# Starting the tiles that TensorE reads at multiples of 256 bytes in SBUF

## The chip, the cores and the metric

The kernel runs on one core of a Trainium2 chip. The metric is device time in microseconds (us): the median of the runs of one program. Beside it stands one profiled execution, with its own time and its span (first to last instruction).

## The reference

One layer of a streaming encoder, for 256 prompt frames and 32 frames of a running stream, so 288 token columns in all, with `D_MODEL` = 2048 and everything in float32:

```python
h = rms_norm(x, g_pre) * (1.0 + scale[:, None]) + shift[:, None]
proj = h @ w_in                      # (2048) x (2048 * 9)
gb, gc, gu, zc, q, k, v, zr, ma, mb = jnp.split(proj, SPLIT_POINTS, axis=-1)
y_conv = gb * causal_conv3(gc * gu) * silu(zc)
y_ret = headRMS(retention(rope(q), rope(k), v)) * silu(zr)
merged = sigmoid(ma) * (y_conv @ w_branch[0]) + sigmoid(mb) * (y_ret @ w_branch[1])
x = x + gate[:, None] * rms_norm(merged @ w_out, g_post)
```

`scale`, `shift` and `gate` come from `silu(c) @ ada_w + ada_b`; new convolution and retention states are also returned.

## The kernel before

**Split products.** The products run in float32r. To keep float32 accuracy each operand is split in a high part (ScalarE copy, L116) and a low part (VectorE subtract, L117). A weight block of 1 MB is loaded into `raw` (L131), split in pieces of 1,024 columns into `whi` and `wlo`, and used by `accumulate` (L151, L152, L154): for each of the k-tiles of a piece, `whi` against the activation's high part, `whi` against its low part, and later `wlo` against the high part. The weights are the stationary operand (128 columns); the activations `hh`/`hl` (later `yh`/`yl`, `ch`/`cl`, `mh`/`ml`) are the moving one (288 columns). There are 9,216 such matmuls of 288 columns, three for each of 3,072 pairs of k-tile and output tile.

**Stages.** (1) `x` is loaded, normalised and transposed (L264); `modulation` (L280) multiplies `ada_w` as a moving operand of 512 columns by a small `cs`; `first_products` computes the first q, k and v columns group by group. (2) The retention loop: `product` for the rest of q, k, v and z, with the steps of `attend` (L397 to L399: `vh`, `vl`, `stateh`, `statel` moving, 256 columns) pushed between them by `step`. (3) The m_b product and the branch of the retention. (4) The convolution branch. (5) m_a, the other branch, and (6) `w_out` with the final norm. TensorE's order is that of the program; weight loads go out on SP's queue, whatever is small on ACT's.

**Where tiles begin.** Pools take SBUF one after the other, each tile from where the last ended, rounded up to 32 bytes. The first tile of the kernel begins at byte 16,512 of each partition. A tile of 288 float32 columns per k-tile, as `hh`, has slices of 1,152 bytes, that is 4.5 x 256, so that its slices begin in turn at two places modulo 256. Starts modulo 256, of the tiles in the argument:

| tile (read by TensorE as) | before | after |
|---|---|---|
| `raw`, `whi`, `wlo` in pool `wp` (weights) | 32 | 0 |
| the extra `raw`, `whi`, `wlo` of pool `start` (buffers 5 and 6 of 6, first stage only) | 0 | 0 |
| `hh`, `hl`, `mh`, `ml`, slices of k even / odd (moving) | 32 / 160 | 0 / 128 |
| `yh`, `yl`, `ch`, `cl`, slices of k even / odd (moving) | 160 / 32 | 0 / 128 |
| `vh`, `vl` (moving, 256 columns) | 128 | 0 |
| `ident`, `gh`, `gl`, `ones` | 128, 160, 160, 160 | 0 |

In the first stage a split piece takes the buffers of `wp` four times and those of `start` twice, in turn (`buffer`, L121 to L125).

Of the kernel before, what the change touches and what calls it, by code (L numbers as in the profile page):

```python
# [10 lines left out]
F32 = mybir.dt.float32  # L11
# [5 lines left out]
P = 128  # L17
D = 2048
NK = D // P
# [5 lines left out]
NH = 8  # L25
# [17 lines left out]
NR = 8  # L43
# [10 lines left out]
PB = dict(v=2, kd=1, pr=1, state=1, qs=1)  # L54
FV = 2 * (len(FIRST) - 2)

DC = TP + P + TS


def tables():  # L60
# [10 lines left out]
    def dec(n):  # L71
        return np.exp((lg.reshape((NH,) + (1,) * np.ndim(n)) * np.asarray(n, f)[None]).astype(np.float64))
# [3 lines left out]
    full = dec(np.abs(j - i)) * (j // CHUNK <= i // CHUNK)  # L76
    d = np.zeros((P, NH, DC), f)
    d[:, :, :TP] = full[:, :P, :].transpose(1, 0, 2)
# [15 lines left out]
def hybrid_step(ctx: ExitStack, tc, x_prompt, x_sample, c_prompt, c_sample, state_conv, state_ret,  # L94
# [4 lines left out]
    V, A, G = nc.vector, nc.scalar, nc.gpsimd  # L99

    const = ctx.enter_context(tc.tile_pool(name="const", bufs=1))
    wp = ctx.enter_context(tc.tile_pool(name="wp", bufs=2))
    big = ctx.enter_context(tc.tile_pool(name="big", bufs=1))
    tmp = ctx.enter_context(tc.tile_pool(name="tmp", bufs=2))
    acc = ctx.enter_context(tc.tile_pool(name="acc", bufs=4, space=PSUM))
    aux = ctx.enter_context(tc.tile_pool(name="aux", bufs=4, space=PSUM))

# [6 lines left out]
    def split(src, hi, lo):  # L114

        A.copy(out=hi, in_=src)  # L116
        V.tensor_tensor(out=lo, in0=src, in1=hi.bitcast(F32), op=ALU.subtract)  # L117
# [48 lines left out]
    def product(w, col, xh, xl):  # L166
# [10 lines left out]
                next(later, None)  # L177
        return [o[:, :T] for o in out]

    ident = const.tile([P, P], F32, name="ident")  # L180
    make_identity(nc, ident)
    neghalf = const.tile([P, 3], F32, name="neghalf")
    V.memset(neghalf, -0.5)
    ones32 = const.tile([P, P], F32, name="ones32")
    V.memset(ones32, 1.0)
    ones = const.tile([P, P], F32R, name="ones")
    V.tensor_copy(ones, ones32)

    def rstd_of(ss, n, width):

        m = tmp.tile([P, 3], F32, name="ms", tag="ms")
        V.tensor_scalar(out=m[:, :width], in0=ss, scalar1=1.0 / n, scalar2=EPS, op0=ALU.mult, op1=ALU.add)
        r = tmp.tile([P, 3], F32, name="rstd", tag="rstd")
        G.tensor_tensor(out=r[:, :width], in0=m[:, :width], in1=neghalf[:, :width], op=ALU.pow)
        return r


    vecs = const.tile([P, NR, NK], F32, name="vecs")
    hh = big.tile([P, NK, T], F32R, name="hh", tag="hh")
    hl = big.tile([P, NK, T], F32R, name="hl", tag="hl")  # L200
    cs = const.tile([P, NK, 12], F32R, name="cs")
    sc = const.tile([P, NK, 2], F32, name="sc")

    early = ExitStack()
    fpool = early.enter_context(tc.tile_pool(name="firsts", bufs=1, side="right", reuse_waits="tile"))
    firsts = fpool.tile([P, 4 * len(FIRST), T], F32, name="firsts")

    rows_of = (P, P, TS)
    with tc.tile_pool(name="start", bufs=1, reuse_waits="tile") as st:
# [25 lines left out]
        V.tensor_tensor(out=sc, in0=cv, in1=sg, op=ALU.mult)  # L235
        V.memset(cs.bitcast(F32), 0.0)
        split(sc, cs[:, :, 4:6], cs[:, :, 6:8])
        ab1 = st.tile([P, NK], F32, name="ab1")
        V.tensor_scalar(out=ab1, in0=vp[:, 2 * NK:3 * NK], scalar1=1.0, scalar2=None, op0=ALU.add)
        xT = st.tile([P, NK, T], F32, name="xT")  # L240

# [4 lines left out]

        def norm_x():

            ss = st.tile([P, 3], F32, name="ss")
            V.memset(ss, 1.0)  # L250
            for g in range(3):
                n = rows_of[g]
                junk = xT.rearrange("p k t -> p (k t)")[:, g * T:g * T + D]
                A.activation(junk[:n], x[:n, g, :], AF.Square, accum_out=ss[:n, g:g + 1])  # L254
            rx = rstd_of(ss, D, 3)
            for g in range(3):
                n = rows_of[g]
                V.tensor_scalar(out=x[:n, g, :], in0=x[:n, g, :], scalar1=rx[:n, g:g + 1], scalar2=None, op0=ALU.mult)
# [81 lines left out]
        h0 = make_h(*GROUPS[0])  # L340
        load_x()
        norm_x()
        for k in range(2):
            turn_x(k)
# [24 lines left out]
    with tc.tile_pool(name="ret", bufs=2, reuse_waits="tile") as rp:  # L369
        rope = rp.tile([P, 2, T], F32, name="rope", bufs=1)  # L370
        A.dma_start(out=rope, in_=rope_t)
        kdec = rp.tile([P, NH, 3], F32, name="kdec", bufs=1)
        A.dma_start(out=kdec, in_=kdec_t)
        qdec = rp.tile([P, NH, TS], F32, name="qdec", bufs=1)
        A.dma_start(out=qdec, in_=qdec_t)
# [16 lines left out]
        def parts(shape, name):  # L392
            return [rp.tile(shape, F32R, name=name + p, bufs=PB[name]) for p in ("h", "l")]

        def add_product(ps, a, b, ai, bi, first, last):

            nc.tensor.matmul(ps, a[0][ai], b[0][bi], start=first, stop=False)  # L397
            nc.tensor.matmul(ps, a[0][ai], b[1][bi], start=False, stop=False)  # L398
            nc.tensor.matmul(ps, a[1][ai], b[0][bi], start=False, stop=last)  # L399
# [18 lines left out]
        def attend(h, q, k, vt, zs):  # L418
# [2 lines left out]
            A.dma_start(out=state, in_=state_ret[0, 0, h])  # L421
            state2 = parts([P, DV], "state")
            split(state, *state2)
            dec = rp.tile([P, DC], F32, name="dec", bufs=1)
            A.dma_start(out=dec, in_=dec_t[:, h, :])

            pk = aux_tile()
# [23 lines left out]
            nc.tensor.matmul(psc[:, 0:TP], k[:, 0:P], q[:, 0:TP], start=True, stop=True)  # L451
            nc.tensor.matmul(psc[:, TP:TP + P], k[:, P:TP], q[:, P:TP], start=True, stop=True)
            nc.tensor.matmul(psc[:TS, TP + P:DC], k[:, TP:T], q[:, TP:T], start=True, stop=True)
            pr = rp.tile([P, DC], F32, name="pr", bufs=1)
            V.tensor_tensor(out=pr[:, :TP + P], in0=psc[:, :TP + P], in1=dec[:, :TP + P], op=ALU.mult)
            V.tensor_tensor(out=pr[:TS, TP + P:], in0=psc[:TS, TP + P:DC], in1=dec[:TS, TP + P:], op=ALU.mult)
            pr2 = parts([P, DC], "pr")
            split(pr[:, :TP + P], pr2[0][:, :TP + P], pr2[1][:, :TP + P])
# [23 lines left out]
            add_product(po[:, DV:2 * DV], pr2, v, (every, slice(TP, TP + P)), (every, 1), False, True)  # L482
            add_product(ps[:TS, 0:DV], qs2, state2, (every,), (every,), True, False)
            add_product(ps[:TS, 0:DV], pr2, v, (few, slice(TP + P, DC)), (few, 2), False, True)
            so = rp.tile([P, 3], F32, name="so")
            V.memset(so, 1.0)
            on = rp.tile([P, 3, DV], F32, name="on", bufs=1)
            src = (po[:, 0:DV], po[:, DV:2 * DV], ps[:TS, 0:DV])
            for g in range(3):
                n = rows_of[g]  # L490
                A.activation(on[:n, g, :], src[g], AF.Square, accum_out=so[:n, g:g + 1])
            ro = rstd_of(so, DV, 3)
            for g in range(3):
                n = rows_of[g]
# [12 lines left out]
        for hp in range(NH // 2):  # L507
            qr = turned(O_Q, 0, "q", hp)
            kr = turned(O_K, 1, "k", hp)
            for f in range(2):  # L510
                h = 2 * hp + f
                v = values(h)
                zs = gates(h)
                while len(side) > 1:
                    step()
                side.append(attend(h, qr[f], kr[f], v, zs))
# [68 lines left out]
    with tc.tile_pool(name="cnv", bufs=2, reuse_waits="tile") as cp:  # L585
        last = cp.tile([P, NK, 4], F32, name="last", bufs=1)
        for q in range(NQ):
# [8 lines left out]
            for f in range(2):  # L596
                kt = 2 * q + f
                g = cp.tile([P, GW], F32, name="g")
# [57 lines left out]
    with tc.tile_pool(name="fin", bufs=2, reuse_waits="tile") as fp:  # L656
        so = fp.tile([P, 3, NQ], F32, name="so", bufs=1)
# [70 lines left out]
```

## Time and profile before

| | us |
|---|---|
| median of 3 runs | 1391.85 (1390.7 to 1396.4) |
| profiled execution, its time | 1392.17 |
| its span | 1390.4 |
| TensorE busy with matmuls, in the span | 1358.9 |
| VectorE, ScalarE busy | 872.3, 611.6 |

A matmul's row gives its start, and a length of some 0.29 us that overlaps with the next; so the cost of one matmul in a stream is read from the distance between two starts. The busy time of TensorE tells only that it hardly ever stood still.

### The profile page before, as it was taken

To read this page: it belongs to the slowest core of one execution; us is meant where nothing else is said; L and a number is where in the kernel's file an instruction comes from. 1 tells how busy PE (TensorE), PEld (TensorE's weight loads), DVE (VectorE), ACT (ScalarE), POOL (GpSimd) and SP (SyncE) were. 2 spreads that over 40 slices of the span, in tenths; PEclk is the share of its full clock that TensorE was granted. 3 is DMA by queue.
4 is the path that set the end of the run, shared out by engine and by line. 5 is a ranking of instruction groups with operands and counts; after the bars stand their busy time and mean duration, and the time that the engine had idled before them with its cause. 6 is when DMAs were issued, how large, how long until landed. Compare 5 with 4: busy or idle time off the path is not lost.

```text
span 1390.4 us, 23832 instructions
## 1 busy us (share of the span) xinstructions
PE 1358.9 (98%) x9978; PEld 1300.1 (94%) x9978; DVE 872.3 (63%) x1426; ACT 611.6 (44%) x885; POOL 9.2 (1%) x16
## 2 busy tenths in 40 slices
PE   4999999999999999999999999999999999999996
PEld 1677899999999999999999999999999999999996
DVE  5888976655545757566767767776555334555443
ACT  6876645544444333333333333333333333334442
POOL 0000000000000000000000000000000000000000
PEclk9999999999999999999999999999999999999998
DMA  9988854344445566575656666566545455557431
GB/s 334 334 302 310 303 175 156 121 158 156 149 159 165 169 196 207 191 241 181 220 185 214 194 202 199 183 201 211 172 155 171 161 171 163 167 168 232 156 105 69
DMA packets 234068, 267.79 MB, mean 193 GB/s; under 512 B 5076, under 2 KB 208132, under 8 KB 233348
## 3 DMA queue, kind: packets, MB, share of 16 engines
q1 hardware_dynamic: 227968, 256.22, 55.8%
q10 hardware_dynamic: 5992, 10.04, 2.7%
q8 instruction: 78, 1.28, 0.4%
q14 instruction: 30, 0.25, 0.0%
HBM read 261.75 MB, written 4.49 MB: 191 GB/s over the span
## 4 chain that ended last, share of the span: by engine, by line
issue 66%; PE 31%; DVE 1%; DMA 0%; ACT 0%; SPq 0%; POOL 0%; DVEq 0%; POOLq 0%; ACTq 0%
PE acc L151 8%; PE acc L154 8%; PE acc L152 8%; PE aux L280 4%; PE aux L397 1%; PE aux L264 1%; PE aux L398 1%; PE aux L399 1%; PE aux L502 0%; DMA x<-in_x_prompt_dram 0%; DVE wlo L117 0%; DVE x L697 0%; PE aux L443 0%; PE aux L451 0%; ACT xT L254 0%
## 5 line engine op out<-in xcount | busy, mean ns | idle before, releaser
L117 DVE TENSOR_TENSOR wlo<-raw,whi 128x1024 fp32r<-128x1024 f32 x448 | 542.1, 1221 | 384.4 <-ACT whi L116 383.8
L116 ACT CAST whi<-raw 128x1024 fp32r<-128x1024 f32 x448 | 464.3, 1050 | 562.8 <-PE acc L152 530.1
L151 PE MATMUL acc<-hh,whi 128*128 128x288 f32 x2304 | 632.1, 296 | 0.0
L152 PE MATMUL acc<-hl,whi 128*128 128x288 f32 x2304 | 631.2, 295 | 0.0
L151 PEld LDWEIGHTS acc<-hh,whi 128*128 128x128 f32 x2304 | 432.5, 188 | 5.0 <-issue 1.7
L152 PEld LDWEIGHTS acc<-hl,whi 128*128 128x128 f32 x2304 | 433.2, 188 | 0.9 <-DVE hl L117 0.3
L154 PE MATMUL acc<-hh,wlo 128*128 128x288 f32 x2304 | 405.4, 293 | 0.0
L154 PEld LDWEIGHTS acc<-hh,wlo 128*128 128x128 f32 x2304 | 340.9, 188 | 0.0
L542 DVE SCALAR_TENSOR_TENSOR gbc<-raw,sc,gbc 128x256 f32<-128x256 f32 x240 | 100.3, 476 | 13.5 <-DMA raw<-in_ada_w_dram 13.5
L152 PE MATMUL acc<-ml,whi 128*128 128x288 f32 x256 | 71.1, 298 | 0.0
L151 PE MATMUL acc<-mh,whi 128*128 128x288 f32 x256 | 70.9, 300 | 0.0
L151 PE MATMUL acc<-yh,whi 128*128 128x288 f32 x256 | 70.0, 296 | 0.0
L152 PE MATMUL acc<-yl,whi 128*128 128x288 f32 x256 | 70.0, 295 | 0.0
L151 PE MATMUL acc<-ch,whi 128*128 128x288 f32 x256 | 70.0, 296 | 0.0
L152 PE MATMUL acc<-cl,whi 128*128 128x288 f32 x256 | 69.5, 294 | 0.0
L280 PE MATMUL aux<-wlo,cs 128*8 128x512 f32 x128 | 51.3, 401 | 0.3
L280 PE MATMUL aux<-whi,cs 128*8 128x512 f32 x128 | 51.6, 403 | 0.0
L151 PEld LDWEIGHTS acc<-mh,whi 128*128 128x128 f32 x256 | 48.3, 189 | 0.1
L152 PEld LDWEIGHTS acc<-cl,whi 128*128 128x128 f32 x256 | 48.3, 189 | 0.0
L152 PEld LDWEIGHTS acc<-ml,whi 128*128 128x128 f32 x256 | 48.1, 188 | 0.1
L152 PEld LDWEIGHTS acc<-yl,whi 128*128 128x128 f32 x256 | 48.2, 188 | 0.0
L151 PEld LDWEIGHTS acc<-yh,whi 128*128 128x128 f32 x256 | 48.1, 188 | 0.1
(188 smaller groups left out, 963.8 us busy)
## 6 DMA issues: line engine op xcount, KB each, us to landing
raw<-in_w_in_dram SPq DMA_DIRECT2D x144, 1024.0 KB, 5.1
raw<-in_ada_w_dram SPq DMA_DIRECT2D x48, 1024.0 KB, 6.5
raw<-in_w_branch_dram SPq DMA_DIRECT2D x32, 1024.0 KB, 5.6
raw<-in_w_out_dram SPq DMA_DIRECT2D x16, 1024.0 KB, 5.6
x<-in_x_prompt_dram SPq DMA_DIRECT2D x2, 1024.0 KB, 5.9
out_dram<-ns SPq DMA_DIRECT2D x16, 128.0 KB, 5.7
x<-in_x_prompt_dram ACTq DMA_DIRECT2D x1, 2048.0 KB, 8.0
out_dram<-x ACTq DMA_DIRECT2D x4, 512.0 KB, 2.8
```

The costliest lines, as they stand in the source:

```text
L116: A.copy(out=hi, in_=src)
L117: V.tensor_tensor(out=lo, in0=src, in1=hi.bitcast(F32), op=ALU.subtract)
L151: nc.tensor.matmul(ps, hi[:, k, fs], xh[:, k0 + k, :], start=first and k == 0, stop=False)
L152: nc.tensor.matmul(ps, hi[:, k, fs], xl[:, k0 + k, :], start=False, stop=False)
L154: nc.tensor.matmul(ps, lo[:, k, fs], xh[:, k0 + k, :], start=False, stop=last and k == n - 1)
L264: nc.tensor.transpose(out=px[:, g * P:g * P + n], in_=x[:n, g, k * P:(k + 1) * P], identity=ident[:n, :n])
L280: nc.tensor.matmul(pm[:8, :width], cs[:, kt, rows_at], w[:, k, :], start=(part == 0 and kt == 0 and w is hi), stop=(part == 1 and kt == NK ...
L397: nc.tensor.matmul(ps, a[0][ai], b[0][bi], start=first, stop=False)
L398: nc.tensor.matmul(ps, a[0][ai], b[1][bi], start=False, stop=False)
L399: nc.tensor.matmul(ps, a[1][ai], b[0][bi], start=False, stop=last)
L542: V.scalar_tensor_tensor(out=ga[:, b], in0=raw[:, k], scalar=sc[:, kt, b:b + 1], in1=ga[:, b], op0=ALU.mult, op1=ALU.add)
```

## The change

Fillers and wider small tiles move the starts; no instruction is added or taken away but in the sizes of tiles. `LINE` is 64 floats (256 bytes), `OFFSET` 32 floats (128 bytes, which takes the first tile from 16,512 to 16,640 = 65 x 256).

```diff
+LINE, OFFSET = 64, 32
...
     const = ctx.enter_context(tc.tile_pool(name="const", bufs=1))
+    tmp = ctx.enter_context(tc.tile_pool(name="tmp", bufs=2))
     wp = ctx.enter_context(tc.tile_pool(name="wp", bufs=2))
     big = ctx.enter_context(tc.tile_pool(name="big", bufs=1))
-    tmp = ctx.enter_context(tc.tile_pool(name="tmp", bufs=2))
...
+    const.tile([P, OFFSET], F32, name="offset")
     ident = const.tile([P, P], F32, name="ident")
-    neghalf = const.tile([P, 3], F32, name="neghalf")
+    neghalf = const.tile([P, LINE], F32, name="neghalf")[:, :3]
-    ones32 = const.tile([P, P], F32, name="ones32")
+    vecs = const.tile([P, NR, NK], F32, name="vecs")
+    ones32 = vecs.rearrange("p r k -> p (r k)")
...
-        m = tmp.tile([P, 3], F32, name="ms", tag="ms")
+        m = tmp.tile([P, LINE], F32, name="ms", tag="ms")
-        r = tmp.tile([P, 3], F32, name="rstd", tag="rstd")
+        r = tmp.tile([P, LINE], F32, name="rstd", tag="rstd")
...
-    sc = const.tile([P, NK, 2], F32, name="sc")
+    sc = const.tile([P, LINE], F32, name="sc")[:, :2 * NK].rearrange("p (k b) -> p k b", b=2)
...
     firsts = fpool.tile([P, 4 * len(FIRST), T], F32, name="firsts")
+    fpool.tile([P, LINE - 8], F32, name="above")
...
-        ab1 = st.tile([P, NK], F32, name="ab1")
+        ab1 = st.tile([P, 2 * NK], F32, name="ab1")[:, :NK]
-            ss = st.tile([P, 3], F32, name="ss")
+            ss = st.tile([P, LINE // 2], F32, name="ss")[:, :3]
...
-        kdec = rp.tile([P, NH, 3], F32, name="kdec", bufs=1)
+        kdec = rp.tile([P, LINE], F32, name="kdec", bufs=1)[:, :3 * NH].rearrange("p (h g) -> p h g", g=3)
-            dec = rp.tile([P, DC], F32, name="dec", bufs=1)
+            dec = rp.tile([P, DC + 32], F32, name="dec", bufs=1)[:, :DC]
-            pr = rp.tile([P, DC], F32, name="pr", bufs=1)
+            pr = rp.tile([P, DC + 32], F32, name="pr", bufs=1)[:, :DC]
-            so = rp.tile([P, 3], F32, name="so")
+            so = rp.tile([P, LINE], F32, name="so", bufs=1)[:, :3]
```

More of the change, by code (lines that the diff above doesn't have):

```diff
@@ L189, in rstd_of @@
     def rstd_of(ss, n, width):
-        m = tmp.tile([P, 3], F32, name="ms", tag="ms")
+        m = tmp.tile([P, LINE], F32, name="ms", tag="ms")
         V.tensor_scalar(out=m[:, :width], in0=ss, scalar1=1.0 / n, scalar2=EPS, op0=ALU.mult, op1=ALU.add)
-        r = tmp.tile([P, 3], F32, name="rstd", tag="rstd")
+        r = tmp.tile([P, LINE], F32, name="rstd", tag="rstd")
         G.tensor_tensor(out=r[:, :width], in0=m[:, :width], in1=neghalf[:, :width], op=ALU.pow)
         return r
-    vecs = const.tile([P, NR, NK], F32, name="vecs")
     hh = big.tile([P, NK, T], F32R, name="hh", tag="hh")
```

## The prediction

> **What bounds the kernel now.** I read the page first (busy shares, the slices, the granted clock, the costliest groups), then TensorE's waits, then its busy time by stretches.
>
> ```profile
> span 1390.4 us, 23832 instructions
> PE 1358.9 (98%) x9978; PEld 1300.1 (94%) x9978; DVE 872.3 (63%) x1426; ACT 611.6 (44%) x885; POOL 9.2 (1%) x16
> PE   4999999999999999999999999999999999999996
> PEclk9999999999999999999999999999999999999998
> L151 PE MATMUL acc<-hh,whi 128*128 128x288 f32 x2304 | 632.1, 296 | 0.0
> ...
> PE aux L264 <- DVE x L258: 9.0, 2, 8.7
> PE aux L244 <- DMA vrows<-in_ada_b_dram: 4.4, 1, 4.4
> ...
> 200.00:300.00 100.00, 100.00 (x734) 1.00 0.44 141
> 500.00:1100.00 600.00, 600.00 (x4543) 1.00 0.60 193
> 1290.00:1377.00 87.00, 86.78 (x653) 1.00 0.31 97
> ```
>
> TensorE is busy 98% of the span at the full granted clock, and its two longest waits, 9.0 and 4.4 us, lie in the first slice. The last three rows are stretches (length, busy time, matmuls in brackets, granted clock, DMA share, GB/s): between 500 and 1,100 us there is no pause, and 600 us over 4,543 matmuls is 132.1 ns each. So the end is set by one number, the distance between the starts of two matmuls of 288 columns, times 9,216: one ns of it is worth 9.2 us. The other engines and the weight loads (DMA share 0.3 to 0.6) have room. Half a per cent of the time, about what a measurement of this kernel tells from no change, is 7.0 us, or 0.76 ns per matmul. The change adds no instruction; it can act only if that distance depends on where tiles begin.
>
> **Does it? Moving operand.** In the rows below (start, length) `whi` meets `hh` and `hl` of an even k (slices from byte 32 modulo 256), then of an odd k (from 160).
>
> ```profile
> 299.62 0.29 PE L151 MATMUL acc<-hh,whi 128*128 128x288 f32 x1
> ...
> 299.88 0.30 PE L151 MATMUL acc<-hh,whi 128*128 128x288 f32 x1
> ...
> 300.15 0.29 PE L151 MATMUL acc<-hh,whi 128*128 128x288 f32 x1
> ...
> 300.41 0.30 PE L151 MATMUL acc<-hh,whi 128*128 128x288 f32 x1
> ...
> 300.68 0.29 PE L154 MATMUL acc<-hh,wlo 128*128 128x288 f32 x1
> ...
> 700.44 0.29 PE L151 MATMUL acc<-hh,whi 128*128 128x288 f32 x1
> ...
> 700.70 0.29 PE L151 MATMUL acc<-hh,whi 128*128 128x288 f32 x1
> ...
> 700.97 0.29 PE L154 MATMUL acc<-hh,wlo 128*128 128x288 f32 x1
> ...
> 47.29 0.80 PE L151 MATMUL acc<-hh,whi 128*128 128x288 f32 x4
> ...
> 1375.71 0.69 PE L154 MATMUL acc<-mh,wlo 128*128 128x288 f32 x4
> ```
>
> At 300 us two matmuls from 32 take 0.26 us (299.62 to 299.88, 300.15 to 300.41) and two from 160 take 0.27 us: 130 against 135 ns each. At 700 us it is again 0.26 and 0.27. The last two rows hold the first and the last of 9,042 pairs of neighbours of 288 columns less than 146 ns apart; over all of them the mean distance is 132.18 ns, 131.02 ns after a start at 32 (4,519 pairs) and 133.33 ns after one at 160 (4,523). The sign is the same in `yh` and `ch`, where the odd k begins at 32, so it follows the place and not the order. Both places are 32 past a multiple of 128; they differ only modulo 256. A slice from 32 ends at 1,184 and touches five stretches of 256 bytes; one from 160 ends at 1,312 and touches six. After the change slices begin at 0 (to 1,152) or 128 (to 1,280): five each, every time.
>
> **Does it? Weights.** The first stage has the weight pieces of both kinds side by side: two of six buffers begin at 0 already, while the moving slices are the same.
>
> ```profile
> 169.67 0.29 PE L151 MATMUL acc<-hh,whi 128*128 128x288 f32 x1
> ...
> 172.86 0.29 PE L151 MATMUL acc<-hh,whi 128*128 128x288 f32 x1
> ...
> 176.06 0.29 PE L151 MATMUL acc<-hh,whi 128*128 128x288 f32 x1
> ...
> 179.18 0.29 PE L151 MATMUL acc<-hh,whi 128*128 128x288 f32 x1
> ...
> 182.30 0.29 PE L151 MATMUL acc<-hh,whi 128*128 128x288 f32 x1
> ```
>
> These are the starts of pieces of 24 matmuls. The two pieces from 169.67 and 172.86 lie at 0 and take 3.19 and 3.20 us, 133.1 ns per matmul; those from 176.06 and 179.18 lie at 32 and take 3.12 us, 130.0 ns. So weights at 0 are the dearer ones, but against moving slices at 32 or 160. What differs is either the place itself or the distance of the two operands, which is 0 or 128 modulo 256 in the cheap pieces and 32 or 160 in the dear ones. After the change weights are at 0 and slices at 0 or 128: the distance of the cheap pieces.
>
> **Other shapes.** Starts of 512-column matmuls (L280, the split weights moving) and of nine of 256 columns (`vh`, `vl` moving):
>
> ```profile
> 27.70 0.40 PE L280 MATMUL aux<-whi,cs 128*8 128x512 f32 x1
> ...
> 29.56 0.40 PE L280 MATMUL aux<-whi,cs 128*8 128x512 f32 x1
> ...
> 30.49 0.40 PE L280 MATMUL aux<-whi,cs 128*8 128x512 f32 x1
> ...
> 238.42 0.28 PE L397 MATMUL aux<-vh,prh 128*128 128x256 f32 x1
> ...
> 239.48 0.28 PE L397 MATMUL aux<-stateh,qsh 128*32 128x256 f32 x1
> ```
>
> Eight matmuls from 27.70 have their moving operand at 0 and take 1.86 us, 232.5 ns each; four from 29.56 have it at 32 and take 0.93 us, 232.5 ns each, the same. The nine of 256 columns begin at 128, their weights at 0 or 128: 1.06 us, 117.8 ns each. A line through these two sizes, (232.5 - 117.8) / 256 = 0.448 ns a column, gives 132.1 ns at 288 columns, what the kernel has now. That speaks against the change.
>
> **The change part by part.** (1) *Moving slices.* Half of the 9,216 matmuls, 4,608, start at 160 today. If the sixth stretch is what costs, each goes from 133.33 to 131.02 ns: 4,608 x 2.31 ns = -10.6 us. From below: all at 130.0 ns, as in the pieces from 176.06, is 9,216 x 2.18 = -20.1 us. From above: all at 133.33 ns is 9,216 x 1.15 = +10.6 us. I take the first value, since the sums over 9,042 pairs are nearer to this work than three pieces. (2) *Weights.* With the distance kept, 0; its bounds are those of (1). (3) *512 and 256 columns.* The 256 matmuls of L280 by the equal rows: 0. The retention's matmuls of 256 columns, 24 for each of eight heads: between 0 and 1.3 ns each (117.8 against 256/288 of 131.02, which is 116.5): at most -0.25 us, taken as 0. (4) *Loads.* In windows of pure weight loading
>
> ```profile
> 13.80:21.80 8.00, 3.67 (x14) 1.00 1.05 387
> 21.90:24.40 2.50, 2.50 (x8) 1.00 1.06 405
> ```
>
> the loads to 32 ran at 387 GB/s and that to 0 at 405, 4.6% faster. It counts only before TensorE is full: from 13.80 us to the row of the first large matmuls at 47.29 are 33.5 us, so at most 33.5 x 0.046 = -1.5 us, at least 0 where the splits on ScalarE and VectorE set the pace; I take -0.5 us. Later the loads have slack, and what is gained is hidden behind TensorE. (5) *VectorE and ScalarE* read and write the same tiles; with 63% and 44% busy, 1% more or less on them is hidden behind TensorE; without that cover 1% of the VectorE row would be 8.7 us. (6) *`so` with one buffer instead of two* makes the next head's memset wait for this head's norm; that norm is issued ahead of it on VectorE's own queue, with a whole product of TensorE between two heads, so 0; if the memset did wait, VectorE's queue would stand behind it, and with it the splits of the next weight pieces, which TensorE needs. (7) *`ones32` inside `vecs`*: the copy to `ones` and the later write of `vecs` are both on VectorE in program order: 0. (8) *`tmp` opened earlier, fillers*: no instruction, 0.
>
> Sum: -10.6 - 0.5 = -11.1 us. The profiled execution took 1392.17 us with a span of 1390.4, so 1.8 us lie outside; it is 0.3 above the median of the runs. The span becomes 1379.3, the time 1381.1, the median some 1380.8; I say 1381.
>
> **The rivals.** *B, no dependence on the place, the distance alone counts.* The difference of 32 and 160 is then that of distances 0 and 128 to the weights, which the change keeps, and the equal 512-column rows and the straight line of sizes hold. TensorE's stream stays at 132.2 ns, 1392.2 - 0.5 = 1391.7, against the median 1391. Against it: the nine 256-column matmuls alternate distances 0 and 128 and cost about one price. [...]
>
> *C, slower: weights at 0 are dear by themselves.* The pieces at 169.67 and 172.86 would then show the rate of the whole kernel: 133.3 ns, 9,216 x 1.15 = +10.6 us, 1402. It decides from a mean of 132.94 ns on (+7 us). For it: those two pieces, at exactly the start that all weights get. Against it: the distance explains them as well, and the 256-column matmuls with weights at 0 or 128 show no such price.
>
> *D, the best cadence everywhere.* The pieces at 176.06 show that 130.0 ns can be held with the operands of today. If the new starts hold it always: -20.1 us, 1372. Against it: at 300 and 700 us the same starts give 132 to 133 ns, so a cadence depends on more than the starts.
>
> **How the numbers follow.** The forecast 0.35, D 0.10, B 0.33, C 0.22. Forecast and D are faster by over 0.5%: 0.45. B is within 0.5%: 0.33. C: 0.22. The likeliest is the forecast, 1381, alone 1377 to 1385 (130.6 to 131.5 ns). The range takes in D's 1372 with 2 us of its own spread and most of C: 1370 to 1401.
>
> **What would show it.** In the changed kernel's trace: matmuls between 500 and 1,100 us, 4,543 now, would be 600 / 0.1310 = 4,580 or more by the forecast, 4,615 by D, 4,540 by B, 4,500 by C; the distances after an even and an odd k would be equal by the forecast and still 131 and 133 by B; the pieces of all six buffers in the first stage would take the same time by all but C. TensorE's waits in the first 47 us should stay. What would make it wrong: a cadence that locks in otherwise than the mean of today's cheap half, since 1 ns is 9.2 us and no row of this trace has both operands at these starts with 288 columns.

## The result and the profile after

The changed kernel takes 1399.09 us (median, 1398.50 to 1399.66) against 1391.94 for the kernel before: a ratio of 1.005, interval 1.0039 to 1.0061. It is slower by 7.2 us. The prediction was 1381; its range, 1370 to 1401, holds the time, its direction is wrong. Some executions, of the kernel before too (1396.4 is one), take 4 to 6 us longer; the profiles of e3, g2, h1 and i1 below are of such executions, with the first large matmul at 49.6 to 50.4 us where all others have it at 46.3 to 47.8, so only their later stages are read, h1's median is of this kind too, and g2's stands between its two times, 1399.28 and 1404.86.

The page of the changed kernel, the rows that answer to those shown of before:

```profile
span 1397.1 us, 23832 instructions
PE 1366.3 (98%) x9978; PEld 1307.9 (94%) x9978; DVE 872.5 (62%) x1426; ACT 611.1 (44%) x885; POOL 9.2 (1%) x16
PE   5999999999999999999999999999999999999996
PEclk9999999999999999999999999999999999999998
```

Its TensorE waits:

```profile
PE aux L269 <- DVE x L263: 8.4, 2, 8.1
PE aux L249 <- DMA vrows<-in_ada_b_dram: 4.5, 1, 4.5
```

Its TensorE by stretches (length, busy time, matmuls, granted clock, DMA share, GB/s):

```profile
200.00:300.00 100.00, 100.00 (x735) 1.00 0.45 142
500.00:1100.00 600.00, 600.00 (x4494) 1.00 0.58 191
1290.00:1377.00 87.00, 87.00 (x656) 1.00 0.34 110
```

The same instructions, the same clock, the same two waits at the start, TensorE as full as before. Only the middle row moved: 4,494 matmuls in 600 us where there were 4,543. Over all pairs of neighbours the distance of two matmuls of 288 columns is now 133.05 ns instead of 132.18: 9,216 x 0.87 = +8.0 us. In these two executions the first large matmul starts 1.0 us earlier (46.29 instead of 47.29):

```profile
46.29 0.80 PE L153 MATMUL acc<-hh,whi 128*128 128x288 f32 x4
```

+8.0 - 1.0 = +7.0 us, against 1397.1 - 1390.4 = 6.7 in the spans.

The timeline of TensorE shows what the stream looks like (start, length). First the changed kernel at 700 us:

```profile
700.09 0.29 PE L153 MATMUL acc<-hh,whi 128*128 128x288 f32 x1
...
700.35 0.30 PE L153 MATMUL acc<-hh,whi 128*128 128x288 f32 x1
...
700.62 0.30 PE L153 MATMUL acc<-hh,whi 128*128 128x288 f32 x1
...
703.29 0.29 PE L153 MATMUL acc<-hh,whi 128*128 128x288 f32 x1
...
706.49 0.29 PE L153 MATMUL acc<-hh,whi 128*128 128x288 f32 x1
```

and the kernel before, there too the starts of 24 matmuls (two output tiles of one split piece):

```profile
701.49 0.29 PE L151 MATMUL acc<-hh,whi 128*128 128x288 f32 x1
...
704.65 0.29 PE L151 MATMUL acc<-hh,whi 128*128 128x288 f32 x1
...
707.81 0.29 PE L151 MATMUL acc<-hh,whi 128*128 128x288 f32 x1
```

24 matmuls take 3.20 us after and 3.16 before, in step, piece after piece. Each product repeats such a period to within a few nanoseconds; averaged over many pieces they are 3,160, 3,173, 3,187 or 3,200 ns, whole multiples of 13.33 ns (237 to 240 of them). I call a period a cadence. Within it the two kinds of slices still differ, and more than before: 131.05 ns after a start at 0 (4,534 pairs), 135.04 after one at 128 (4,530).

The two kernels did not differ from the start. In stretches of the retention, of the long products behind it, and of the branch behind m_a (`ch`; before, the last 7 us already belong to `w_out`), before:

```profile
300.00:450.00 150.00, 150.00 (x1116) 1.00 0.48 155
720.00:1060.00 340.00, 340.00 (x2577) 1.00 0.60 193
1195.00:1275.00 80.00, 80.00 (x607) 1.00 0.57 178
```

and after:

```profile
300.00:450.00 150.00, 150.00 (x1115) 1.00 0.48 159
720.00:1060.00 340.00, 340.00 (x2545) 1.00 0.58 191
1195.00:1275.00 80.00, 80.00 (x602) 1.00 0.53 169
```

In the retention 1,116 against 1,115: both hold 3,200. They part at the first product that has `yh` and `yl` moving. Before:

```profile
471.58 0.29 PE L151 MATMUL acc<-yh,whi 128*128 128x288 f32 x1
...
474.77 0.29 PE L151 MATMUL acc<-yh,whi 128*128 128x288 f32 x1
...
481.11 0.29 PE L151 MATMUL acc<-hh,whi 128*128 128x288 f32 x1
...
484.27 0.29 PE L151 MATMUL acc<-hh,whi 128*128 128x288 f32 x1
```

After:

```profile
469.91 0.29 PE L153 MATMUL acc<-yh,whi 128*128 128x288 f32 x1
...
473.11 0.29 PE L153 MATMUL acc<-yh,whi 128*128 128x288 f32 x1
...
479.51 0.29 PE L153 MATMUL acc<-hh,whi 128*128 128x288 f32 x1
...
482.71 0.29 PE L153 MATMUL acc<-hh,whi 128*128 128x288 f32 x1
```

Before, `yh` runs at 3.19 us per 24, and the `hh` product behind it comes back at 3.16; every later `hh` product, up to 1,167 us, has that too. After, all stay at 3.20. Before, `yh` begins at 160 where `hh` begins at 32, 128 bytes out of step with it; the change put both at 0. The experiments ask whether that is the cause, and what multiples of 256 have to do with it.

### The profile page after: what moved, and what is told of

It is laid out like the page before. It is cut to its first block, busy times and chain, and to the rows that moved or that the text cites. A ratio compares the mean times of both kernels' runs of the same rounds, so it can differ in the third digit from the quotient of the medians.

```text
span 1397.1 us, 23832 instructions
## 1 busy us (share of the span) xinstructions
PE 1366.3 (98%) x9978; PEld 1307.9 (94%) x9978; DVE 872.5 (62%) x1426; ACT 611.1 (44%) x885; POOL 9.2 (1%) x16
## 4 chain that ended last, share of the span: by engine, by line
issue 67%; PE 31%; DVE 1%; DMA 0%; ACT 0%; SPq 0%; POOL 0%; DVEq 0%; POOLq 0%; ACTq 0%
PE acc L153 8%; PE acc L154 7%; PE acc L156 7%; PE aux L285 4%; PE aux L402 1%; PE aux L269 1%; PE aux L403 1%; PE aux L404 1%; PE aux L507 0%; DMA x<-in_x_prompt_dram 0%; DVE wlo L119 0%; DVE x L702 0%; PE aux L448 0%; PE aux L456 0%; SPq L219 0%
## 5 line engine op out<-in xcount | busy, mean ns | idle before, releaser
L156 PE MATMUL acc<-hh,wlo 128*128 128x288 f32 x2304 | 410.4, 296 | 0.0
L153 PEld LDWEIGHTS acc<-ch,whi 128*128 128x128 f32 x256 | 48.4, 189 | 0.0
```

Of the source, the lines that this page charges most:

```text
L153: nc.tensor.matmul(ps, hi[:, k, fs], xh[:, k0 + k, :], start=first and k == 0, stop=False)
L156: nc.tensor.matmul(ps, lo[:, k, fs], xh[:, k0 + k, :], start=False, stop=last and k == n - 1)
```

## The experiments

The table has every layout that was run. Starts are modulo 256: W of the weights, M of `hh`, `hl`, `mh`, `ml`, Y of `yh`, `yl`, `ch`, `cl`, each for an even k; the slice of an odd k lies 128 further, but where "all at" says that slices lie 1,280 bytes apart and so all begin alike. The counts are matmuls in the three stretches above; the last column is the cadence of 24 in ns, in the `hh` products behind the retention and in the `yh` and `ch` products.

| run | W, M, Y | median us | ratio (interval) | counts | hh; yh, ch |
|---|---|---|---|---|---|
| before | 32, 32, 160 | 1391.9 | 1 | 1116, 2577, 607 | 3,160; 3,187 and 3,173, once 3,253 |
| after | 0, 0, 0 | 1399.09 | 1.005 (1.0039 to 1.0061) | 1115, 2545, 602 | 3,200; 3,200 |
| e1_w0_h32 | 0, 32, 64 | 1398.25 | 1.0053 (1.0037 to 1.0068) | 1115, 2554, 604 | 3,187; 3,187 |
| e2_w32_h0 | 32, 0, 64 | 1393.82 | 1.0013 (1.0004 to 1.0023) | 1122, 2566, 605 | 3,173; 3,187 |
| e3_w64_h64 | 64, 64, 0 | 1396.58 | 1.0039 (1.0024 to 1.0054) | 1114, 2546, 605 | 3,200 and 3,160; 3,187, some 3,160 |
| e4_w0_h0_y32 | 0, 0, 32 | 1398.77 | 1.0051 (1.0034 to 1.0068) | 1113, 2526, 605 | 3,200, 3,160 and 3,267; 3,187 |
| f1_d160_d96 | 32, 192, 128 | 1403.0 | 1.0083 (1.0054 to 1.0113) | 1111, 2540, 602 | 3,207; 3,200 |
| f2_hl_shift | 32, 32 (`hl` 160), 0 (`yl` 128) | 1407.01 | 1.0112 (1.0083 to 1.0142) | 1119, 2503, 602 | 3,187 and 3,253; 3,200 |
| f3_pitch1280 | 32, all at 32, Y 160 in turn | 1392.18 | 1.0014 (1.0003 to 1.0026) | 1126, 2578, 593 | 3,160; 3,173 and 3,253 |
| g1_all_d0 | 32, all at 32, all at 32 | 1387.56 | 0.997 (0.9959 to 0.9982) | 1125, 2578, 610 | 3,160; 3,160 |
| g2_d32_d64 | M all 32 and Y all 64 past W | 1402.07 | 1.0075 (1.0051 to 1.0098) | 1112, 2545, 610 | 3,200; 3,160 and 3,173 |
| g3_d96_d128 | M all 96 and Y all 128 past W | 1391.22 | 0.9997 (0.9986 to 1.0007) | 1123, 2573, 602 | 3,160, some 3,200; 3,200 |
| h4_pitch_w0 | 0, all at 0, all at 0 | 1387.22 | 0.9967 (0.9955 to 0.998) | 1124, 2578, 610 | 3,160; 3,160 |
| i1_after_y128 | 0, 0, 128 | 1393.28 | 1.0012 (1.0001 to 1.0024) | 1114, 2571, 607 | 3,160 (28 products) and 3,200 (19); 3,187 and 3,173 |
| i2_before_y32 | 32, 32, 32 | 1403.7 | 1.0082 (1.0065 to 1.0099) | 1115, 2524, 610 | 3,200 (21), 3,267 (18) and 3,160 (8); `yh` 3,200 and 3,267, `ch` 3,160 |

All 9,216 matmuls of 288 columns are in e4's record; its 2,526 is so low because some of its products between 720 and 1,060 us run at 3,267.

**Other starts for weights and slices (e1 to e4).** Fillers alone move the starts of the kernel before; Y moves along in each of them, so no operand moves quite alone. Of e1 and e4:

```diff
 e1:
+    const.tile([P, 56], F32, name="offset")     # first in const: everything + 224
+    gap.tile([P, 8], F32, name="gap")           # own pool between wp and big: hh + 32
+    tmp.tile([P, 40], F32, name="tgap", bufs=1) # yh further
 e4:
+    const.tile([P, 56], F32, name="offset")
+    tmp.tile([P, 40], F32, name="tgap", bufs=1)
```

> The kernel before with fillers alone: weights (whi, wlo) at 0 modulo 256, hh, hl and mh, ml slices at 32 and 160, yh and ch slices at 64 and 192. Weights theory (weights at a multiple of 64 bytes are dear whatever moves): 133.3 ns a matmul in the hh stages, 500 to 1,100 us, some 4,500 matmuls there, and the kernel near 1399 us. Moving theory (moving slices at a multiple of 64 are dear, weights do not matter): 131.7 ns in the hh stages, some 4,540, and 133.3 in the ch stage (1,100 to 1,280 us), kernel near 1393 us.

> The kernel before with fillers alone: weights at 32, hh and hl slices at 0 and 128, yh and ch slices at 64 and 192. Weights theory: 131.7 ns in the hh stages as before, near 1392 us. Moving theory: 133.3 ns in the hh and in the ch stages, near 1399 to 1402 us.

> The kernel before with fillers alone: weights at 64, hh and hl slices at 64 and 192, yh and ch slices at 0 and 128: all at multiples of 64 but not of 256. Both theories, if the unit is 64 bytes: 133.3 ns everywhere, near 1399 to 1402 us. If the unit is 128 or 256 bytes, 64 is like 32: 131.7 ns in the hh stages, near 1392 us.

> The kernel before with fillers alone: weights at 0 and hh, hl slices at 0 and 128 as in the change, but yh and ch slices at 32 and 160, and none of the change's other edits (small vectors, so with one buffer, the order of the pools). If the starts are all there is to the change: 133.3 ns in the hh stages. In the ch stage the weights theory has 133.3, the moving theory 132.2 as before. If one of the other edits makes the loss: 131.7 ns and 1392 us.

All four are slower than before. The stretch from 720 us in e1 and in e2:

```profile
720.00:1060.00 340.00, 340.00 (x2554) 1.00 0.58 192
```

```profile
720.00:1060.00 340.00, 340.00 (x2566) 1.00 0.60 194
```

e4 has W and M of the change and none of its edits of `vecs`, `so`, `dec` or the small tiles: 1398.77 against 1399.09. So fillers alone can make such a loss. That the other edits cost nothing is not shown by this, since e4 has another Y and other cadences than the change, and its equal time is partly chance. But in the change's trace the lengthened period accounts for the loss (+8.0 us, where the spans differ by 6.7), and TensorE's waits are the old ones. A place at 0 is not what the slow layouts share: e1 with the weights at 0 lies at 1398, e2 with `hh` at 0 at 1394, e3 with neither at 0 at 1397.

**Distances and slices (f1 to f3).** f1 moves `hh` on by 160, f2 the low halves by 128, f3 makes the slices begin alike:

```diff
 f1:
+    gap.tile([P, 40], F32, name="gap")
 f2:
+    big.tile([P, 32], F32, name="hgap")         # between hh and hl; ygap likewise
 f3:
-PB = dict(v=2, kd=1, pr=1, state=1, qs=1)
+PB = dict(v=1, kd=1, pr=1, state=1, qs=1)
-    hh = big.tile([P, NK, T], F32R, name="hh", tag="hh")
+    hh = big.tile([P, NK, T + 32], F32R, name="hh", tag="hh")[:, :, :T]   # hl, mh, ml likewise
```

> The kernel before with fillers alone: weights at 32, hh and hl slices at 192 and 64 (distance of moving to weights 160, then 32, modulo 256), yh and ch slices at 128 and 0 (distance 96, then 224). Distance theory (the distance alone sets which cadences a stage can take; at 0 it is 3,160 or 3,200 ns for 24 matmuls, elsewhere a single one): one cadence in each stage, between 3,173 and 3,187, never 3,160 or 3,200; near 1393 to 1398 us. Place theory (each operand's own start counts): hh slices at multiples of 64 give 3,200, and 1399 us or more.

> The kernel before with fillers alone: hh slices at 32 and 160 as before, hl slices at 160 and 32, so that the high and the low half of one k have distances 0 and 128; yh and ch at 0 and 128, yl and cl at 128 and 0 (distances 224 and 96). Distance theory: the pattern of distances is new, so a cadence of its own, one per stage, between 3,120 and 3,200. Place theory by 256-byte stretches: as before, 3,160, 1392 us.

> The kernel before with hh, hl, mh and ml slices 1,280 bytes apart instead of 1,152, so that every slice begins at 32 like the weights (distance 0 for all); v of attend has one buffer instead of two to make room, which lengthens the retention stage by a little. Forecast's theory (a slice that touches six stretches of 256 bytes is dear): 131.0 ns for every matmul, 3,144 for 24, and the even and the odd k alike. Distance theory: no alternation between distances 0 and 128 remains; if that alternation makes the dear half, 3,120 (130.0 ns) in the hh stages and some 1378 us; if a lock on 13.33 ns makes it, still 3,160 or 3,200.

f1 and f2 are, with i2, the slowest layouts. (f1's 3,207 is no whole multiple: 240.5 steps of 13.33.) f3 holds 3,160 in the retention too, 1,126 matmuls from 300 to 450, and gives the gain back where its `yh` and `ch`, still in turn at 160 and 32, run at 3,173 and 3,253:

```profile
1195.00:1275.00 80.00, 80.00 (x593) 1.00 0.56 173
```

**Is the cadence fixed by the layout? (f4 and g4).** The change and the kernel before, each with one tiny transpose ahead of each of 71 products:

```diff
+        nc.tensor.transpose(out=aux_tile()[:32, :32], in_=ident[:32, :32], identity=ident[:32, :32])
```

> The changed kernel with one transpose of 32 by 32 on TensorE ahead of each of the 71 products after the retention loop; all starts stay. Distance theory with two cadences at distance 0: the extra instruction restarts the stream, and some products come back at 3,160 ns for 24 instead of 3,200; 71 transposes cost 71 x 0.1 = 7 us at most. If the starts at 0 fix the rate (weights or place theory): 3,200 in every product, as in the change.

> The kernel before with one transpose of 32 by 32 on TensorE ahead of each of the 71 products after the retention loop; all starts as before. Lock theory (at distances 0 and 128 the stream can hold 3,160, 3,200 or 3,267 for 24 matmuls, and what came last decides): the hh and mh products show these same three values, though the starts are at 32 and not at 0. Place theory: the hh products stay at 3,160 or show values that the changed kernel with the same transposes did not.

Three products of f4, one after the other, the first two pieces of each:

```profile
733.74 0.29 PE L153 MATMUL acc<-hh,whi 128*128 128x288 f32 x1
...
736.94 0.29 PE L153 MATMUL acc<-hh,whi 128*128 128x288 f32 x1
...
746.84 0.29 PE L153 MATMUL acc<-hh,whi 128*128 128x288 f32 x1
...
750.00 0.29 PE L153 MATMUL acc<-hh,whi 128*128 128x288 f32 x1
...
759.86 0.29 PE L153 MATMUL acc<-hh,whi 128*128 128x288 f32 x1
...
763.12 0.29 PE L153 MATMUL acc<-hh,whi 128*128 128x288 f32 x1
```

3.20, then 3.16, then 3.26 us, with the same tiles at the same addresses. Over all `hh` products f4 has 3,160 seven times, 3,200 fourteen times, 3,267 twenty-six times; g4, with the starts of before, eight, twelve and twenty-seven times. So a layout does not fix the cadence: several are open to it, and something other than the starts chooses. In the `hh` products the two layouts have the same choice. In the `yh` and `ch` products they have not: f4 has 3,160, 3,200 and 3,267 there, g4 3,173 and once 3,253. Most of the added time, 1428.27 and 1426.07, is the transposes' own: the product of 3.20 above takes 13.10 us from start to start (733.74 to 746.84) where four pieces make 12.80, some 0.3 us for a transpose, where 0.1 had been expected, and 21 us for 71; the rest is in the longer cadences.

**One distance for all (g1 to g3, h4).** All eight activation tiles with slices 1,280 bytes apart (as in f3, with `sw` in one buffer to make room), so that each stage behind the first has one distance from weights to slices: 0 in g1 and h4, others in g2 and g3.

```diff
 h4 (g1 has no offset):
+    const.tile([P, 56], F32, name="offset")
+    tmp.tile([P, 32], F32, name="tgap", bufs=1)
-    yh = ybig.tile([P, NK, T], F32R, name="yh", tag="yh")
+    yh = ybig.tile([P, NK, T + 32], F32R, name="yh", tag="yh")[:, :, :T]   # all eight
```

> The kernel before with all eight activation tiles (hh, hl, yh, yl, ch, cl, mh, ml) in slices 1,280 bytes apart that begin at 32 like the weights: distance 0 for every 288-column matmul; to make room v and sw of the retention have one buffer. Distance theory: the hh stages as with the pitch of 1,280 alone (3,160 for 24 matmuls), and the yh and ch stages come from 3,253 down to 3,160 too: 1,536 matmuls x 3.9 ns = -6 us against that run, near 1386 us. If what happens at the entry of a stage decides (lock theory): 3,160, 3,200 or 3,267 in any stage.

> As the run with distance 0 everywhere, but hh, hl, mh, ml slices all 32 bytes past the weights modulo 256, yh, yl, ch, cl slices all 64 past. Distance theory: one cadence each, not 3,160 and 3,200; between 3,173 and 3,253, so 1393 to 1405 us. If only the alternation of two distances matters: as at distance 0.

> As the run with distance 0 everywhere, but hh, hl, mh, ml slices all 96 bytes past the weights modulo 256, yh, yl, ch, cl slices all 128 past. Distance theory with a unit of 128 bytes: 128 is like 0, so 3,160 or 3,200 in the yh and ch stages, and another cadence at 96. With a unit of 256 bytes: a third value at 128.

> As the run with distance 0 everywhere (slices 1,280 bytes apart), but weights and all slices start at 0 instead of 32 modulo 256: the change's starts, without its alternation of 0 and 128. If one distance for all slices is what holds the cheap cadence: 3,160 throughout, as at 32, and about 1 us less at the head since raw is at 0: near 1386.5 us, faster than both kernels. If starts at 0 make 3,200: near 1397 us.

The three stretches of h4:

```profile
300.00:450.00 150.00, 150.00 (x1124) 1.00 0.49 160
720.00:1060.00 340.00, 340.00 (x2578) 1.00 0.58 192
1195.00:1275.00 80.00, 80.00 (x610) 1.00 0.58 188
```

g1 and h4 hold 3,160 in every stage from the retention on and are faster than both kernels; h4's 1387.22 is 0.8% below the change (1387.22 / 1399.09 = 0.9915, from the two medians, not measured side by side). In h4 the weights of `wp` and all slices begin at 0, in g1 at 32: 0.3 us apart. So, with one distance for all, a start at a multiple of 256 neither gains nor costs in the stream. The distance has a say: at 32 `hh` is at 3,200, at 96 mostly at 3,160, `ch` at 64 near 3,160 and at 128 at 3,200. g2 and g3 show no order by size in that. Where even and odd k alternate, the distance goes with a set of cadences in all runs with full weight loads: products at 0 and 128 past the weights ran at 3,160, 3,200 or 3,267 (`hh` in before, after, e3, e4, f4, g4, i1 and i2, `yh` and `ch` in after, f4 and i2), products at 128 and 0 at 3,173, 3,187 or 3,253 (`yh` and `ch` in before, f3, g4 and i1). By that the change moved `yh` and `ch` from the second set to the first and left `hh` in its own.

**A single disturbance, and a smaller weight load (h1 to h3).** h1 and h2 put one and two transposes into the change at about 662 us; h3, from the kernel before, loads 32 of the 128 weight columns, and so writes 32 rows, in the matmuls of `hl` and all but the last of a sum of `wlo`; it leaves out the rest of these low-order products:

```diff
 h3:
-            nc.tensor.matmul(ps, hi[:, k, fs], xl[:, k0 + k, :], start=False, stop=False)
+            nc.tensor.matmul(ps[:32], hi[:, k, fs][:, :32], xl[:, k0 + k, :], start=False, stop=False)
...            (the matmul of wlo likewise)
```

> The changed kernel with one single transpose of 32 by 32 on TensorE ahead of the first product of the convolution stage (at some 680 us); nothing else differs, all starts at 0. Lock theory: from there on the stream can settle on 3,160, 3,200 or 3,267 for 24 matmuls and stay there through the hh products of that stage, 500 us or 158 such groups: -6.3, 0 or +10.6 us against the change. Place theory: 3,200 as in the change, 1399 us.

> As the run with one transpose, but two of them at the same point. Lock theory: again one of the three cadences for the rest of the stage, and not necessarily the same as with one. Place theory: 3,200, 1399 us.

> The kernel before where the second and the third kind of matmul (whi against the low part, wlo against the high part) load 32 columns of weights instead of 128 and write 32 rows, except for the last one of a sum: that part of the low-order products is left out. The moving operand and the number of matmuls stay. If the weight load that runs beside a matmul makes the stalls: the distances of matmuls whose neighbour loads 32 columns fall from 131 or 133 ns towards 120 to 125, and the cadence with them. If the stalls are the moving operand's alone: 3,160 or 3,200 for 24 matmuls as before.

h1 and h2 came back to 3,200 behind the transposes (2,544 and 2,545 matmuls from 720 us; medians 1404.39 and 1399.66 us): one push at that place does not change the cadence. h3 took 1381.74 us, in one run. Its `hh` products hold 3,147 ns for 24, that is 236 steps of 13.33 ns; its `yh` and `ch` products have pieces between 3,120 and 3,157, some 3,129 on average:

```profile
300.00:450.00 150.00, 150.00 (x1127) 1.00 0.50 160
720.00:1060.00 340.00, 340.00 (x2592) 1.00 0.60 192
1195.00:1275.00 80.00, 80.00 (x616) 1.00 0.61 200
```

Its mean is 131.1 ns a matmul, and the sign of the two kinds of slices turned: 131.6 ns after a start at 32, 130.6 after one at 160. So the dearer kind of slice is no property of the place, and the weight load beside a matmul, or the number of rows written, takes part in the cadence; h3 makes both smaller and does not separate them. The 120 to 125 ns that the first of the two expectations named were a guess of mine, worked out from no run, and did not come: the lowest mean over a stage is 130.4 (3,129 / 24, in `yh` and `ch`). The smaller load with its smaller output changed the distance between matmuls by some 0.5 ns in `hh` (3,147 / 24 = 131.1 against 3,160 / 24 = 131.7).

**The step between two products (i1 and i2).** The decisive pair: of the operands of 288-column matmuls behind the first stage only `yh`, `yl`, `ch`, `cl` move, by 128 bytes; in the change out of step with `hh`, in the kernel before into step. (Other tiles that lie behind the filler move along.)

```diff
 i1, against the change:
+    ybig.tile([P, 32], F32, name="ygap")
-            dec = rp.tile([P, DC + 32], F32, name="dec", bufs=1)[:, :DC]
+            dec = rp.tile([P, DC], F32, name="dec", bufs=1)
 i2, against the kernel before:
+    tmp.tile([P, 32], F32, name="tgap", bufs=1)
```

> The changed kernel with yh, yl, ch and cl 128 bytes further (slices at 128, 0 instead of 0, 128), paid for by the filler of dec; weights, hh and hl stay at 0. If the relation of yh to hh makes the loss: yh products at 3,173 to 3,200, and the hh products from 478 us on at 3,160 as in the kernel before; near 1391 us. If the starts at 0 make it: 3,200 throughout, 1399 us.

> The kernel before with 128 bytes of filler, so that yh, yl, ch and cl begin at 32 as hh does (slices at 32, 160 instead of 160, 32); weights, hh and hl stay at 32. If the relation of yh to hh makes the loss: 3,200 throughout from 478 us on, near 1399 us, though no tile begins at a multiple of 256 that did not before. If the starts at 0 make it: 3,160 in the hh products, near 1392 us.

The `hh` product behind the first `yh` product, in i1:

```profile
484.62 0.29 PE L153 MATMUL acc<-hh,whi 128*128 128x288 f32 x1
...
487.78 0.29 PE L153 MATMUL acc<-hh,whi 128*128 128x288 f32 x1
```

and in i2:

```profile
477.77 0.29 PE L152 MATMUL acc<-hh,whi 128*128 128x288 f32 x1
...
480.97 0.29 PE L152 MATMUL acc<-hh,whi 128*128 128x288 f32 x1
```

3.16 and 3.20 us: the cadences have changed places. The traces bear this out product by product. Eight times a product with `yh` is followed by one with `hh`, six times with nothing between them. In these six `hh` comes in at 3,160 in before and in i1, whether `yh` ran at 3,173, 3,187 or 3,253. In the change and in i2 it keeps what `yh` had, 3,200 or 3,267. So out of step, each `yh` product sends the stream to 3,160; in step, the stream carries on the 3,200 that it had in the retention.

Other instructions can change a cadence too. In i2, between two `hh` products (the two of 512 columns belong to the final `gate`, and such a pair comes after every fifth product there):

```profile
711.97 0.29 PE L152 MATMUL acc<-hh,whi 128*128 128x288 f32 x1
...
715.23 0.29 PE L152 MATMUL acc<-hh,whi 128*128 128x288 f32 x1
...
725.03 0.39 PE L551 MATMUL aux<-gh,ones 128*128 128x512 f32 x1
725.26 0.39 PE L552 MATMUL aux<-gl,ones 128*128 128x512 f32 x1
725.49 0.29 PE L152 MATMUL acc<-hh,whi 128*128 128x288 f32 x1
...
728.69 0.29 PE L152 MATMUL acc<-hh,whi 128*128 128x288 f32 x1
```

3.26 us ahead of them, 3.20 behind, with the same tiles. From 660 to 1,160 us the `hh` cadences of i1, i2, e3 and e4 change only there and behind the 16 transposes at some 1,060 us; in before and in the change the same matmuls change nothing.

i1 gets 1399.09 - 1393.28 = 5.8 of the change's 7.2 us back, not all of it, since 19 of its 47 `hh` products still run at 3,200. i2 loses 11.7 us, more than the change, since 18 of its run at 3,267. `hh` and the weights have the same starts in i1 as in the change and in i2 as in before. So what the change took away was the 128 bytes by which `yh` was out of step with `hh`. With `hh` the weights begin alike in all four, so whether it is the distance of `yh` to `hh` or to the weights that counts was not tested.

## Why the prediction was wrong, by its steps

**(1) Moving slices, -10.6 us: the step that failed.** The rows of 131.02 and 133.33 ns were right, and so was their sign in `yh` and `ch`; the reading, that a sixth stretch of 256 bytes costs 2.31 ns, was not. After the change every slice touches five stretches, and those at 128 take 135.04 ns; in h3 the slices with six were the faster ones, 130.6 against 131.6 ns. The two figures are parts of one cadence, whose sum is what is fixed. In place of -10.6 us stands +8.0: the `hh` products behind 480 us went from 3,160 to 3,200, 40 / 24 = 1.7 ns per matmul, and the retention, which had been at 3,200, stayed. What the sum had wrong is that a matmul has a price of its own which its start sets. The place where it could have been seen is the prediction's own D: "the same starts give 132 to 133 ns, so a cadence depends on more than the starts". Followed to where that changes, the trace of before had it: 3,200 up to the first `yh` product, 3,160 behind it. The term was priced by sums over 9,042 pairs, which mix both.

**(2) Weights, 0 with the distance kept.** The premise that the distance counts and not the place is borne out by g1 and h4 (distance 0, weights at 32 and at 0: 3,160 in both) and by g2 (the weights at 32 as in g1, `hh` 32 past them: 3,200). That the change keeps the distances holds for `hh` and `mh` alone: in `yh` and `ch` they were 128 and 0 for even and odd k and became 0 and 128. And a kept distance does not keep the rate: `hh` has the distances of before, and 3,200 for 3,160.

**(3) Other shapes, 0.** Right: 512 columns took 231.3 ns after and 231.9 before, 256 columns some 119 and 118. They run in bursts of at most 51.

**(4) Loads, -0.5 us, between -1.5 and 0.** Not shown. The row of 46.29 is 1.0 us earlier than that of 47.29, but with the change's starts f4 and h2 have 47.34 and 47.01, and with those of before g4 and h3 have 47.83 and 46.70.

**(5) to (8), 0.** Nothing contradicts it: TensorE's two waits at the start stayed (8.4 for 9.0, 4.5 for 4.4), the retention kept its count (1,115 for 1,116), and i1, which has nearly all of these edits, is within 0.12% of before. No run has the change's starts without them.

**The rivals.** B's number, no change in the stream, did not come, though its premise was nearer than the forecast's. C's number came, 133.05 ns and 4,494 matmuls where it said 133.3 and 4,500, but not its reason: in h4 weights at 0 run at 131.7 ns. D's 130.0 ns held over a stage in no layout with full weight loads; its pieces at 176.06 do two k-tiles for four output tiles, where a product's do four for two, and from 194.9 us on the trace of before has 3,160 in pieces of that second kind. Of the sign posts, 4,494 against 4,580 refuted the forecast at once; the pieces of all six buffers in the first stage did take the same time, 3.16 us from 164.83 to 190 us, which spoke against C; the pair distances, 131.05 and 135.04, were expected by none. What came is what the last sentence of the prediction names, a cadence that locks in otherwise.

**What stays open.** Why the periods are multiples of 13.33 ns (all but f1's and the `yh` and `ch` of h3), and by what rule an old cadence, a distance or the matmuls in between choose the next. i1 and i2 show the effect of 128 bytes between `yh` and `hh`; e1 to e4, where it is other amounts, give 3,160 to 3,267 without a rule that I can see. Nor is it shown how short the distance can get: no run here held less than 130 ns per matmul over a stage, the lowest being 130.4 (3,129 / 24, h3's `yh` and `ch`) and, with full weight loads, 131.7 (3,160 / 24).

## What to carry to other kernels

In a stream without pauses a difference between two kinds of instructions can be a pattern of one joint cadence and not a cost of either kind (here the slices at 160 were the dearer ones in the kernel before, 133.33 ns against 131.02, and the cheaper ones in h3, 130.6 against 131.6): before pricing it per instruction, see whether the period of the whole pattern is fixed, and whether the same addresses show other periods elsewhere in the trace. Judge a layout by the counts of whole stages, and look at how the operands of successive products stand to each other, not only at each start. Slices all at one distance from the weights (here 1,280 bytes apart, at the weights' own start) held the best cadence with full weight loads in every stage from the retention on, 1387.2 us; a round address alone did nothing (1387.22 us with weights and slices at 0, 1387.56 at 32).

## What the runs showed of the hardware that was not expected

- TensorE's stream of 288-column matmuls, each with its own weight load (9,978 loads for 9,978 matmuls of all sizes), has several stable speeds at the same addresses: in f4's `hh` products 3,160, 3,200 and 3,267 ns per 24, 3.4% from the first to the last. The layouts spread from 1387.2 to 1407.0 us with the same instructions.
- One 32 x 32 transpose ahead of each product was enough to move the speed of the products (`hh` at 3,160, 3,200 and 3,267 ns in 7, 14 and 26 products of f4 and in 8, 12 and 27 of g4), and a single one, at one of these places, was not (h1, 3,200 behind it as in the change). Two 512-column matmuls between products moved it in i1, i2 (from 3.26 to 3.20 us) and e4, and not in before and after (3,160 and 3,200 on both sides).
- With 32 instead of 128 weight columns loaded, and rows written, in two matmuls of three the `hh` stream was only some 0.5 ns per matmul faster than the best cadence: 3,147 ns for 24 instead of 3,160.
